# Moving the last S5 scan, its readout and its relay behind the first attention head

## The chip, the cores and the metric

The kernel runs on one core of a Trainium2 chip. The metric is the device time of one execution in microseconds (us). The kernel before takes 1720.06 us (median of 3 runs, 1719.47 to 1720.97). The engines are named as the profile names them: PE (matmul) with its weight loads PEld, DVE (vector), ACT (scalar), POOL (GpSimd) and SP, which here only issues DMAs. Each engine works through its own list of instructions in order.

## The reference

One layer over 512 tokens of width 1024. Cut to what matters here:

```
proj = rmsnorm(x) @ w_in                       # columns: q, k, v (512 each) and u (512)
att  = chunked_attention(rmsnorm(q), rmsnorm(k), v, rel_bias)      # 8 heads of 64
ssm  = s5_mixer(u)                             # diagonal complex scan, then gelu, then a gate
h    = x + concat(rmsnorm(att), rmsnorm(ssm)) @ w_out
h    = h + memory_attention(rmsnorm(h), rmsnorm(mem))              # 256 memory tokens, 4 heads
h    = h + peer_ffn(rmsnorm(h))                # product-key experts
```

In the mixer, y = Re(C x) + d u is read out of the scanned state x, then `y = gelu(y)` and `y = y * sigmoid(y @ w_glu + b_glu)`. The change touches only the order of work inside the mixer, the attention heads and the norm of the memory; what is computed stays the same.

## The kernel before

The program has a front (norm, projections, S5, attention, memory attention) and the expert part. The change lies in the front, between about 137 and 320 us of the span; the expert part fills the rest.

Large products in single precision are made of three passes: `load_split` (L97) brings a weight tile in (tile `wraw`, SP queue, 3 buffers), ACT rounds it (`whi`, L108), DVE or POOL forms the rest (`wlo`, L110), and PE runs L124 to L126 on them (4 buffers of `whi` and of `wlo`). A weight buffer comes free when the last product that reads it is done.

The S5 scan works in four quarters, `scan(0)` to `scan(3)` (L466). A quarter is eight small products into two PSUM banks (`pb`, L472), some sixteen DVE instructions (multiplications L479 to L484, eight `tensor_tensor_scan` L487, multiplications L491 to L496), and the scanned state `XX`. `readout(q)` (L498) is twelve products (`py`, L504 to L506) and a copy on ACT into `Ug` (L507). `relay` (L511) sends `Ug` through HBM to change its layout: eight DMAs write `Ys` (L515, four from the SP queue, four from ACT's), and one DMA on ACT's queue reads `yT` back (L518). `glu_in` (L632) then runs gelu over `yT` on ACT (L634) and splits it (`yh`, `yl`), and `glu` uses it.

An attention head (`att_head`, L669) is a few score products (`pS`, L684), a DVE step with the bias and the row maximum (L685), exp on ACT (L686), transposes on PE (L689), a copy on DVE (`apt`, L690), products with v (`po`, L694) and a scaling (`att`, L698). `mem_in` (L582) normalises the memory (`norm_T`, L166: a square on ACT, a scaling on DVE, transposes `ntp` on PE, the split `Mh`, `Ml` on ACT and DVE). `mem_k(0)` and `mem_k(1)` multiply it by the two halves of `w_mk` (`pv` from `Mh`, 48 products each), and the result leaves PSUM by ACT: a copy `kN` (L597) and two squares `kj` (L599) for each of two token blocks.

PSUM is handed out by tag: two banks under "g" (`pv`, `pz`, `pk`), two under "s" (`pb`, `py`, `ntp`, `po`), four under "a" (`pS`, `pbc` and transposes). The two banks of `mem_k(1)` are those of `mem_k(0)`, so its first product waits for the `kN` and `kj` of `mem_k(0)`.

What is written first in the program has the higher priority; a scheduler in the compiler fixes each engine's list before the run. The string `PLAN` gives the order from the heads on: digits are heads, m the memory norm, i `glu_in`, g `glu`, k K and v V the halves of the memory keys and values. The scratch tile `xn` of a norm comes from a pool of four tiles (`t4`), which the scan's matrices `MT` and states `XX` use too; `p8` is a pool of four larger tiles, which the transposed input `XT` fills until the product for v is done.

Of the kernel before, what the change touches and what calls it, by code (L numbers as in the profile page):

```python
# [9 lines left out]
F32 = mybir.dt.float32  # L10
# [25 lines left out]
    _o += _w  # L36
NVEC = _o
NB8 = 10
PLAN = 'im012kK34g5v6V7'
POG = 0  # L40
LK = "v"
LV = "gv"
# [16 lines left out]
def setup(tc, es):  # L59
    c = Ctx()  # L60
# [6 lines left out]
    V, S, G, P = c.V, c.S, c.G, c.P  # L67
# [17 lines left out]
    def t4(name, dt=F32, w=1024):  # L85
        return c.tp.tile([128, w], dt, tag="t4", name=name, bufs=4)

    def small(name, shape, dt=F32, bufs=4):
        return c.tp.tile(shape, dt, tag=name, name=name, bufs=bufs)
# [73 lines left out]
        for b, pv in zip(blocks, pvs):  # L163
            evac(b, 0, pv)

    def norm_T(src, blocks, gain, hl, keep=None, gb=None):  # L166
        if gb is None:
            gb = t4("gb")
            nc.sync.dma_start(gb, gain.partition_broadcast(128))
        for b in blocks:  # L170
            xn = t4("xn")
            ss = small("nss", [128, 2])
            S.activation(xn, src(b), AF.Square, accum_out=ss[:, 0:1])
            rpow(ss[:, 1:2], ss[:, 0:1], 1.0 / 1024)
            V.scalar_tensor_tensor(xn, src(b), ss[:, 1:2], gb, op0=OP.mult, op1=OP.mult)  # L175
            if keep:
                keep(b, xn)
            for half in range(2):
                pt = pst("s", "ntp")
                for q in range(4):  # L180
                    k = half * 4 + q
                    P.transpose(pt[:, q * 128:(q + 1) * 128], xn[:, k * 128:(k + 1) * 128], c.ident)
                pt3 = pt.rearrange("p (k t) -> p k t", k=4)
                hi, lo = hl[0].part(half, b), hl[1].part(half, b)
                S.activation(hi, pt3, AF.Copy)
                c.nt_ins = V.tensor_tensor(lo, pt3, hi, op=OP.subtract).ins
# [29 lines left out]
def front(tc, I, c):  # L216
    nc, V, S, G, P, cp, tp = c.nc, c.V, c.S, c.G, c.P, c.cp, c.tp
    pst, t2, t4, small, vc, rpow, mm3, gemmT, gemmN, norm_T = (
        c.pst, c.t2, c.t4, c.small, c.vc, c.rpow, c.mm3, c.gemmT, c.gemmN, c.norm_T)
# [3 lines left out]
    with tc.tile_pool(name="f1", bufs=1) as f1:  # L223
# [15 lines left out]
        gb = b8([128, 1024], "gb")  # L239
# [226 lines left out]
        def scan(q, MT):  # L466
            pb = [pst("s", "pb") for _ in range(2)]
            s_ = slice(q * 4, q * 4 + 4)
            v3 = lambda a: a.rearrange("p (g c) -> p g c", g=4)
            for h in range(2):  # L470
                for z in range(4):
                    P.matmul(pb[h][:, z * 128:(z + 1) * 128], MT[h][:, q % 2 * 4 + z], Ug[:, q * 4 + z], start=True, stop=True)  # L472
            X = t4("XX").rearrange("p (h g c) -> p h g c", h=2, g=4)
            XX.append(X)
            G.memset(X[:, :, :, 0:1], 0.0)
            br, bi = v3(pb[0]), v3(pb[1])
            tr, ti = Tr[:, s_], Ti[:, s_]
            x0, x1, zr_, zi_ = [v3(f(n_)) for n_, f in (("x0", p2), ("x1", p2), ("zr", a2), ("zi", a2))]
            V.tensor_tensor(x0, br, tr, op=OP.mult)  # L479
            V.tensor_tensor(x1, bi, ti, op=OP.mult)  # L480
            V.tensor_tensor(zr_, x0, x1, op=OP.add)
            V.tensor_tensor(x0, bi, tr, op=OP.mult)
            V.tensor_tensor(x1, br, ti, op=OP.mult)
            V.tensor_tensor(zi_, x0, x1, op=OP.subtract)  # L484
            for z in (zr_, zi_):
                for g in range(4):
                    V.tensor_tensor_scan(z[:, g], mag4[:, q * 4 + g:q * 4 + g + 1].broadcast_to([128, 128]), z[:, g], 0.0,  # L487
                                         op0=OP.mult, op1=OP.add)
            n_ = slice(0, 127)
            T = V.tensor_tensor  # L490
            T(x0, zr_, tr, op=OP.mult)  # L491
            T(x1, zi_, ti, op=OP.mult)
            T(X[:, 0, :, 1:128], x0[:, :, n_], x1[:, :, n_], op=OP.subtract)
            T(x0, zr_, ti, op=OP.mult)
            T(x1, zi_, tr, op=OP.mult)
            T(X[:, 1, :, 1:128], x0[:, :, n_], x1[:, :, n_], op=OP.add)  # L496

        def readout(q):  # L498
            py = pst("s", "py")
            for z in range(4):  # L500
                g = q * 4 + z
                X = XX[q]
                o = py[:, z * 128:(z + 1) * 128]
                P.matmul(o, Mx[:, g], Ug[:, g], start=True, stop=False)  # L504
                P.matmul(o, CAr[:, g], X[:, 0, z], start=False, stop=False)
                P.matmul(o, CAi[:, g], X[:, 1, z], start=False, stop=True)  # L506
            S.activation(Ug[:, q * 4:q * 4 + 4].rearrange("p g c -> p (g c)"), py, AF.Copy)  # L507
# [3 lines left out]
        def relay():  # L511
            Ys = c.dr.tile([32, 16, 4, 128], F32, name="Ys")
            for a in range(2):
                for j in range(4):
                    (nc.sync if j % 2 else nc.scalar).dma_start(  # L515
                        Ys.rearrange("(g a) ch j c -> a j ch g c", a=2)[a, j], Ug[64 * a + 16 * j:64 * a + 16 * j + 16])
            yT.append(b8([128, 4, 512], "yT"))
            nc.scalar.dma_start(yT[0], Ys.rearrange("(m g) ch j c -> (g ch) m (j c)", m=4))  # L518
# [11 lines left out]
        for i in range(2):  # L530
# [9 lines left out]
            if i == 0:  # L540
                local()
                MT = min_T(0, Mn)
                scan(0, MT)
            else:
# [4 lines left out]
                MT = min_T(1, Mn)  # L549
# [14 lines left out]
            rhl.append((rh, rl))  # L564
        vN = b8([128, 4, 512], "vN")
        gemmN([[I["w_v"][i] for i in range(4)]], XT, range(4), lambda b, ct, p: S.activation(vN[:, b], p, AF.Copy), leng=V)
        scan(3, MT)
        readout(2)
        readout(3)
        relay()  # L570
        for i, (rh, rl) in enumerate(rhl):
            for m in range(4):
                pbc = pst("a", "pbc")
# [6 lines left out]
        M = []  # L580

        def mem_in():  # L582
            M.extend(pair(c.p8, "M", 256))
            me = c.p8([128, 2, 1024], "me", F32)
            nc.scalar.dma_start(me, I["mem"].rearrange("(b p) d -> p b d", p=128))
            norm_T(lambda b: me[:, b], range(2), I["gkv"], M)

        mkv = {}

        def mem_k(ct):  # L590
            if ct == 0:
                mkv["kN"] = b8([128, 2, 1024], "kN")
                mkv["ks"] = small("ks", [128, 2, 4], bufs=1)
            kN, ks = mkv["kN"], mkv["ks"]

            def ev(b, _, p):
                S.activation(kN[:, b, ct * 512:(ct + 1) * 512], p, AF.Copy)  # L597
                for e in range(2):
                    S.activation(t2("kj")[:, :256], p[:, e * 256:(e + 1) * 256], AF.Square,  # L599
                                 accum_out=ks[:, b, ct * 2 + e:ct * 2 + e + 1])  # L600
            c.gemmK([I["w_mk"][ct * 4 + i] for i in range(4)], M, range(2), ev, leng=LK)
            if ct == 0:
                return
            mkT = mkv["k"] = b8([128, 8, 256], "mkT")
            dg = []
            for b in range(2):
                rk = small("rk", [128, 4])
                rpow(rk, ks[:, b], 1.0 / 256)
                d_ = t2("dg").rearrange("p (h t) -> p h t", h=4)
                V.tensor_tensor(d_, ident.unsqueeze(1).broadcast_to([128, 4, 128]),  # L610
                                rk.unsqueeze(2).broadcast_to([128, 4, 128]), op=OP.mult)
                dg.append(d_)
            for hd in range(4):
                pk = pst("g", "pk")
                for m in range(2):
                    for b in range(2):
                        P.matmul(pk[:, m * 256 + b * 128:m * 256 + (b + 1) * 128], kN[:, b, hd * 256 + m * 128:hd * 256 + (m + 1) * 128],
                                 dg[b][:, hd], start=True, stop=True)
                for m in range(2):
                    S.activation(mkT[:, hd * 2 + m], pk[:, m * 256:(m + 1) * 256], AF.Copy, scale=vc("gmk", m))  # L620

        def mem_v(ct):
            if ct == 0:
                mkv["v"] = b8([128, 2, 1024], "mv")
            c.gemmK([I["w_mv"][ct * 4 + i] for i in range(4)], M, range(2),
                  lambda b, _, p: S.activation(mkv["v"][:, b, ct * 512:(ct + 1) * 512], p, AF.Copy), leng=LV)
# [71 lines left out]
            V.tensor_tensor(att[:, :, h * 64:(h + 1) * 64], po[:, :256].rearrange("p (b d) -> p b d", b=4),  # L698
                            sm[:, 1].unsqueeze(2).broadcast_to([128, 4, 64]), op=OP.mult)

        todo = {"m": mem_in, "i": glu_in, "g": glu, "k": lambda: mem_k(0), "K": lambda: mem_k(1), "v": lambda: mem_v(0), "V": lambda: mem_v(1)}
        for o in PLAN:
            att_head(int(o)) if o.isdigit() else todo[o]()
        sums = small("sums", [128, 4])
# [525 lines left out]
```

## Time and profile before

| | |
|---|---|
| median of 3 runs | 1720.06 us |
| the profiled execution, its own time | 1718.78 us |
| its span, from first to last instruction | 1717.0 us |
| PE busy | 1663.6 us (97%) |
| DVE busy | 1348.9 us (79%) |
| ACT busy | 722.2 us (42%) |
| POOL busy | 687.6 us (40%) |
| mean granted TensorE clock | 0.988 |

A share of busy time is a mean over the whole span. The page's line of PEclk over 40 slices shows tenths of full speed; it stands at 9 nearly everywhere, so what matters for this change is read from windows of the stretch around 140 to 180 us, where the transposed input has been used up, the scan ends and the heads begin. The chain that ended last gives PE 80% of the span and DVE 13%.

### The profile page before, as it was taken

How to read it: one execution, taken by the hardware profiler on the slowest of the kernel's cores; microseconds unless marked ns; L12 is line 12 of the kernel's file. 1: busy time of each engine (PE TensorE's matmuls, PEld its weight loads, DVE VectorE, ACT ScalarE, POOL GpSimd, SP SyncE). 2: the span in 40 equal slices, each digit the busy share in tenths (PEclk: the TensorE clock that was granted, in tenths of full speed). 3: DMA queues.
4: the chain of work that ended last, by engine and by line, in shares of the span. 5: the costliest groups of instructions: out<-in, count | busy, mean ns of one | idle time of the engine just before them, and what ended most of it. 6: DMA issues, size and time to landing. Idle time of an engine off the chain costs nothing.

```text
span 1717.0 us, 24874 instructions
## 1 busy us (share of the span) xinstructions
PE 1663.6 (97%) x8929; PEld 1447.8 (84%) x8929; DVE 1348.9 (79%) x2699; ACT 722.2 (42%) x1185; POOL 687.6 (40%) x598
## 2 busy tenths in 40 slices
PE   7998999999999989999999999999999999999998
PEld 6776778877787879999998999999999999988886
DVE  7989564654579989987797878787778787889977
ACT  4343673433333247887433333333333333333332
POOL 5130032441477854100255545445444444455431
PEclk9998999999999989999999999999999999999999
DMA  6422433220522237777647998998898888899995
GB/s 203 112 57 92 136 117 121 94 86 13 184 96 71 94 130 224 232 239 234 224 146 263 341 348 323 331 335 298 325 325 327 328 326 313 325 333 348 346 402 213
DMA packets 159852, 388.70 MB, mean 226 GB/s; under 512 B 14440, under 2 KB 74856, under 8 KB 159600
## 3 DMA queue, kind: packets, MB, share of 16 engines
q1 hardware_dynamic: 107504, 212.83, 36.7%
q0 software_dynamic: 36864, 134.23, 21.5%
q10 hardware_dynamic: 15360, 40.05, 6.8%
q8 instruction: 70, 1.15, 0.3%
q14 instruction: 54, 0.44, 0.1%
HBM read 351.48 MB, written 35.26 MB: 225 GB/s over the span
## 4 chain that ended last, share of the span: by engine, by line
PE 80%; DVE 13%; DMA 2%; POOL 2%; issue 2%; ACT 1%; SPq 0%; ACTq 0%; DVEq 0%; POOLq 0%
PE acc L1105 28%; PE pa L124 10%; PE pa L126 9%; PE pa L125 9%; PE pw L1036 3%; PE pv L124 3%; PE pv L126 3%; PE pv L125 3%; DMA act<-Ad 1%; DVE ca L900 1%; PE po L694 1%; DVE ex L921 1%; PE pS L684 1%; DVE xn L175 1%; DVE wlo L110 1%
## 5 line engine op out<-in xcount | busy, mean ns | idle before, releaser
L108 ACT ACTIVATE whi<-wraw 128x1024 fp32r<-128x1024 f32 (+1 forms) x332 | 349.1, 1054 | 392.3 <-PE pa L125 204.4
L110 DVE TENSOR_TENSOR wlo<-wraw,whi 128x1024 fp32r<-128x1024 f32 (+1 forms) x278 | 344.1, 1238 | 51.9 <-ACT whi L108 51.6
L124 PE MATMUL pa<-PTh,whi 128*128 128x384 f32 x1024 | 353.9, 346 | 3.2 <-ACT act L1063 3.2
L126 PE MATMUL pa<-PTh,wlo 128*128 128x384 f32 x1024 | 347.3, 339 | 3.8 <-POOL wlo L110 3.8
L125 PE MATMUL pa<-PTl,whi 128*128 128x384 f32 x1024 | 346.4, 338 | 0.0
L974 POOL DMA_INDIRECT vg<-in_peer_v_dram,ei x128 | 184.3, 1440 | 212.4 <-DVE X L975 195.9
L964 POOL DMA_INDIRECT ug<-in_peer_u_dram,ei x128 | 181.2, 1416 | 200.2 <-DVE ug L965 179.3
L1105 PE MATMUL acc<-wlo,ah 128*128 128x512 f32 x768 | 236.8, 391 | 3.4 <-DVE wlo L110 3.4
L1105 PE MATMUL acc<-whi,ah 128*128 128x512 f32 x768 | 236.7, 392 | 0.8 <-ACT whi L108 0.8
L1105 PE MATMUL acc<-whi,al 128*128 128x512 f32 x768 | 236.6, 391 | 0.0
L124 PEld LDWEIGHTS pa<-PTh,whi 128*128 128x128 f32 x1024 | 194.2, 190 | 6.8 <-ACT act L1063 3.5
L126 PEld LDWEIGHTS pa<-PTh,wlo 128*128 128x128 f32 x1024 | 194.2, 190 | 5.1 <-POOL wlo L110 5.1
L125 PEld LDWEIGHTS pa<-PTl,whi 128*128 128x128 f32 x1024 | 194.4, 190 | 3.3
L965 DVE SCALAR_TENSOR_TENSOR ug<-ug,X 128x1024 f32<-128x1024 f32 x128 | 152.9, 1222 | 41.0 <-DMA ug<-in_peer_u_dram,ei 40.8
L1093 ACT ACTIVATE ah<-act 128x384 fp32r<-128x384 f32 x128 | 67.2, 526 | 266.2 <-PE acc L1105 218.5
L1105 PEld LDWEIGHTS acc<-wlo,ah 128*128 128x128 f32 x768 | 144.4, 188 | 35.3 <-DVE wlo L110 3.8
L975 DVE SCALAR_TENSOR_TENSOR X<-vg,dots,X 128x1024 f32<-128x1024 f32 x128 | 164.2, 1283 | 9.6 <-DMA vg<-in_peer_v_dram,ei 5.5
L110 POOL TENSOR_TENSOR wlo<-wraw,whi 128x1024 fp32r<-128x1024 f32 x54 | 131.5, 2443 | 99.8 <-ACT whi L108 99.8
L1105 PEld LDWEIGHTS acc<-whi,al 128*128 128x128 f32 x768 | 144.4, 188 | 31.1
L1105 PEld LDWEIGHTS acc<-whi,ah 128*128 128x128 f32 x768 | 143.3, 188 | 26.4 <-ACT whi L108 1.6
L1039 ACT ACTIVATE stg<-pw 128x256 f32<-128x256 f32 x192 | 104.8, 682 | 27.9 <-PE pw L1036 22.7
L1101 DVE TENSOR_TENSOR al<-act,ah 128x384 fp32r<-128x384 f32 x128 | 72.4, 566 | 37.5 <-ACT ah L1093 37.4
(383 smaller groups left out, 2637.1 us busy)
## 6 DMA issues: line engine op xcount, KB each, us to landing
wraw<-in_ut_dram SPq DMA_DIRECT2D x128, 512.0 KB, 5.4
wraw<-in_peer_v_dram SPq DMA_DIRECT2D x128, 512.0 KB, 6.5
Wd<-stg SPq DMA_DIRECT2D x24, 1024.0 KB, 5.9
wt<-Wd ACTq DMA_DIRECT2D x32, 768.0 KB, 7.7
wraw<-in_w_pq_dram SPq DMA_DIRECT2D x16, 512.0 KB, 3.3
h<-in_x_dram SPq DMA_DIRECT2D x8, 512.0 KB, 6.8
wraw<-in_w_qk_dram SPq DMA_DIRECT2D x8, 512.0 KB, 3.9
wraw<-in_w_mk_dram SPq DMA_DIRECT2D x8, 512.0 KB, 4.2
```

The source lines that it names most:

```text
L108: S.activation(hi, raw, AF.Copy)
L110: ins = leng.tensor_tensor(lo, raw, hi, op=OP.subtract).ins
L124: P.matmul(out, lhs[0], rhs[0], start=first, stop=False)
L125: P.matmul(out, lhs[0], rhs[1], start=False, stop=False)
L126: P.matmul(out, lhs[1], rhs[0], start=False, stop=last)
L964: G.indirect_dma_start(out=ug, out_offset=None, in_=I["peer_u"], in_offset=IOX(ap=ei[:, k:k + 1], axis=0))
L965: V.scalar_tensor_tensor(ug, ug, 1.0, c.X0, op0=OP.mult, op1=OP.mult, accum_out=dots[:, k:k + 1])
L974: G.indirect_dma_start(out=vg, out_offset=None, in_=I["peer_v"], in_offset=IOX(ap=ei[:, k:k + 1], axis=0))
L975: V.scalar_tensor_tensor(a0, vg, dots[:, k:k + 1], a0, op0=OP.mult, op1=OP.add)
L1039: S.activation(stg[e][:, :, q * 8 + hf * 4:q * 8 + hf * 4 + 4].rearrange("p i t -> p t i"), pw.rearrange("p (t i) -> p t i", t=4)[:, :, e ...
L1101: c.v_ins = V.tensor_tensor(al, a, ah, op=OP.subtract).ins
L1105: P.matmul(acc[b * 2 + d], l[:, b * 128:(b + 1) * 128], v[r][:, d * 512:(d + 1) * 512], start=n == 0 and l is ah and r == 0, stop=n == 127 ...
```

## The change

Two edits. First, the last quarter's scan, its readout and the relay leave their place ahead of the heads; they become an entry `s` of the plan, behind head 0, and `glu_in` (i) moves from the first place behind head 2. Second, the memory norm takes the pool `p8` for its gain and its scratch tile: a fourth tile `gx` there holds the gain in one half (loaded over ACT's queue instead of SP's) and the scratch of both blocks in the other half; no `t4` tile is used there any more.

```
-PLAN = 'im012kK34g5v6V7'
+PLAN = 'm0s12ikK34g5v6V7'
...
-    def norm_T(src, blocks, gain, hl, keep=None, gb=None):
+    def norm_T(src, blocks, gain, hl, keep=None, gb=None, xn=None):
...
+        scratch = xn
         for b in blocks:
-            xn = t4("xn")
+            xn = t4("xn") if scratch is None else scratch
...
-        scan(3, MT)
         readout(2)
-        readout(3)
-        relay()
...
-            norm_T(lambda b: me[:, b], range(2), I["gkv"], M)
+            gx = c.p8([128, 2, 1024], "gx", F32)
+            nc.scalar.dma_start(gx[:, 0], I["gkv"].partition_broadcast(128))
+            norm_T(lambda b: me[:, b], range(2), None, M, gb=gx[:, 0], xn=gx[:, 1])
...
-        todo = {"m": mem_in, "i": glu_in, "g": glu, ...}
+        def scan_out():
+            scan(3, MT)
+            readout(3)
+            relay()
+
+        todo = {"s": scan_out, "m": mem_in, "i": glu_in, "g": glu, ...}
```

The lists of the engines differ from about 139 us on and have the same order again from within the product with `w_out` on. Three places follow. Line numbers of the kernel after lie one to five higher or up to two lower than before for the same operation.

ACT, from the relay's read (`yT` from `Ys`) to the first copy of the memory keys (`kN`); `asb` is the exp of a head. Before, the gelu over `yT` stands between exps of heads 0 and 1, and the next exp comes behind `kN`:

```order
L518 DMA yT<-Ys 128x4x512
L686 ACTIVATE asb,asm<-asb,asm 128x256
L686 ACTIVATE asb,asm<-asb,asm 128x512
L634 ACT_TABLE_LOAD
L634 ACTIVATE yT<-yT 128x2048
L636 ACTIVATE yh<-yT 128x512 x4
L108 ACTIVATE whi<-wraw 128x1024
L597 ACTIVATE kN<-pv 128x512
L599 ACTIVATE kj,ks<-pv 128x256 x2
L108 ACTIVATE whi<-wraw 128x1024
L686 ACT_TABLE_LOAD
```

These are the same operations after, with exps of heads 2 and 3:

```order
L519 DMA yT<-Ys 128x4x512
L686 ACTIVATE asb,asm<-asb,asm 128x384
L686 ACTIVATE asb,asm<-asb,asm 128x256
L686 ACTIVATE asb,asm<-asb,asm 128x128
L686 ACTIVATE asb,asm<-asb,asm 128x256
L634 ACT_TABLE_LOAD
L634 ACTIVATE yT<-yT 128x2048
L686 ACT_TABLE_LOAD
L686 ACTIVATE asb,asm<-asb,asm 128x512
L636 ACTIVATE yh<-yT 128x512 x4
L597 ACTIVATE kN<-pv 128x512
L599 ACTIVATE kj,ks<-pv 128x256 x2
```

The gelu stands ahead of the first `kN` in both lists; after, the second table load and one exp have moved between the gelu and `kN`, and the split `whi` of a weight has left that place.

PE, where the readout of a quarter (`py`) meets the score products of the heads (`pS` from `kT`, `qT`). Before, the readouts of quarters 2 and 3 follow the first four score products, and `mem_k(0)` (`pv` from `Mh`) comes behind them:

```order
L575 MATMUL pbc<-rl,selr 128x512
L684 MATMUL pS<-kT,qT 128x512
L684 MATMUL pS<-kT,qT 128x384
L684 MATMUL pS<-kT,qT 128x128
L684 MATMUL pS<-kT,qT 128x512
L504 MATMUL py<-Ug,Mx 128x128
L505 MATMUL py<-XX,CAr 128x128
L506 MATMUL py<-XX,CAi 128x128
```

All 24 products of the two readouts stood there, with eleven transposes, two score products and two GEMM products between. After, the readout of quarter 3 begins behind the second half of that scan's products (`pb`) and the last two products of `mem_k(0)`:

```order
L473 MATMUL pb<-Ug,MT 128x128 x4
L125 MATMUL pv<-wlo,Mh_1429 128x512
L126 MATMUL pv<-whi,Ml_1430 128x512
L505 MATMUL py<-Ug,Mx 128x128
L689 MATMUL pS<-ident,asb 128x128 x4
L694 MATMUL po<-vN,apt 128x64 x4
L684 MATMUL pS<-kT,qT 128x384
L506 MATMUL py<-XX,CAr 128x128
L689 MATMUL pS<-ident,asb 128x128 x3
L684 MATMUL pS<-kT,qT 128x256
L507 MATMUL py<-XX,CAi 128x128
```

What moved in front of it are all 48 products of `mem_k(0)` and the rest of head 0; its products now stand between work of heads 1 and 2. Some 30 rows further on in the list after, `mem_k(1)` begins:

```order
L684 MATMUL pS<-kT,qT 128x128
L694 MATMUL po<-vN,apt 128x64 x3
L684 MATMUL pS<-kT,qT 128x512
L689 MATMUL pS<-ident,asb 128x128 x4
L684 MATMUL pS<-kT,qT 128x256
L124 MATMUL pv<-whi,Mh_1429 128x512
```

Between the readout of quarter 3 and this place the list after holds only work of heads 1 to 4; in the list before, products of `mem_k(0)` and `mem_k(1)` stand between the heads' pieces all the way.

DVE, in the first half of the last quarter's scan (`pb` times the tables `Tr` and `Ti`). Before:

```order
L480 TENSOR_TENSOR x_1379<-pb,Ti 128x512
L481 TENSOR_TENSOR zr<-x_1378,x_1379 128x512
L482 TENSOR_TENSOR x_1378<-pb,Tr 128x512
L483 TENSOR_TENSOR x_1379<-pb,Ti 128x512
L487 SCALAR_TENSOR_TENSOR zr<-mag_387,zr 128x128 x4
L484 TENSOR_TENSOR zi<-x_1378,x_1379 128x512
```

It stood in one piece ahead of head 0's bias steps, and the splits `wlo` of `w_mk` for `mem_k(1)` came much later. After:

```order
L110 TENSOR_TENSOR wlo<-wraw,whi 128x1024
L480 TENSOR_TENSOR x_1523<-pb,Tr 128x512
L110 TENSOR_TENSOR wlo<-wraw,whi 128x1024 x2
L481 TENSOR_TENSOR x_1524<-pb,Ti 128x512
L482 TENSOR_TENSOR zr<-x_1523,x_1524 128x512
L110 TENSOR_TENSOR wlo<-wraw,whi 128x1024
L483 TENSOR_TENSOR x_1523<-pb,Tr 128x512
L484 TENSOR_TENSOR x_1524<-pb,Ti 128x512
L488 SCALAR_TENSOR_TENSOR zr<-mag_387,zr 128x128 x4
L485 TENSOR_TENSOR zi<-x_1523,x_1524 128x512
```

Head 0 and the memory's splits have moved ahead of this place, and the four splits `wlo` for `mem_k(1)` stand among the scan.

## Rows read from the trace of the kernel before

**Rows 1.** Windows of 10 us: busy us (instructions) of each engine, PEclk, DMA share, GB/s
```profile
150.00:160.00 10.00, 5.24 (x8) 1.69 (x7) 9.79 (x18) 0.00 (x0) 0.26 (x2) 0.50 0.14 50
160.00:170.00 10.00, 9.17 (x47) 8.03 (x48) 9.93 (x27) 4.14 (x10) 0.92 (x1) 0.73 0.01 2
```

**Rows 2.** Timeline, PE: start us, us, line, out<-in, forms, xcount [idle before <-releaser]
```profile
142.53 2.05 PE L472 MATMUL pb<-Ug,MT 128*128 128x128 f32 x16
...
149.45 5.79 PE L684 MATMUL pS<-kT,qT 64*128 64x512 f32 x8 [1.60 <-DVE rv L120]
160.01 0.77 PE L504 MATMUL py<-Ug,Mx 128*128 128x128 f32 x2 [4.76 <-DVE x L482]
...
165.26 0.43 PE L504 MATMUL py<-Ug,Mx 128*128 128x128 f32 x2
...
171.81 0.39 PE L506 MATMUL py<-XX,CAi 128*128 128x128 f32 x2
172.03 0.60 PE L182 MATMUL ntp<-ident,xn 128*128 128x128 f32 x4
172.39 0.48 PE L126 MATMUL pv<-whi,Ml 128*128 128x512 f32 x1
...
315.36 1.03 PE L182 MATMUL ntp<-ident,xn 128*128 128x128 f32 x8
```

**Rows 3.** Timeline, PE, in the dense stretch behind
```profile
186.60 2.34 PE L694 MATMUL po<-vN,apt 128*128 128x64 f32 x20
188.87 1.13 PE L684 MATMUL pS<-kT,qT 64*128 64x384 f32 x4
189.93 0.50 PE L125 MATMUL pv<-wlo,Mh 128*128 128x512 f32 x1
...
190.50 0.40 PE L124 MATMUL pv<-whi,Mh 128*128 128x512 f32 x1
190.74 0.40 PE L125 MATMUL pv<-wlo,Mh 128*128 128x512 f32 x1
```

**Rows 4.** Timeline, DVE
```profile
136.68 1.23 DVE L110 TENSOR_TENSOR wlo<-wraw,whi 128x1024 fp32r<-128x1024 f32 x1 [2.40 <-ACT whi L108]
...
153.03 1.28 DVE L175 SCALAR_TENSOR_TENSOR xn<-me,nss,gb 128x1024 f32<-128x1024 f32 x1
...
160.38 1.36 DVE L487 TENSOR_TENSOR_SCAN zr<-mag,zr 128x128 f32<-128x128 f32 x4
161.65 0.67 DVE L484 TENSOR_TENSOR zi<-x,x 128x512 f32<-128x512 f32 x1
162.24 0.68 DVE L685 CUSTOM_DVE_ANT_0 asb<-pS,bt 128x512 f32<-128x512 f32 x1
...
168.72 0.68 DVE L496 TENSOR_TENSOR XX<-x,x 128x508 f32<-128x508 f32 x1
...
169.92 0.68 DVE L186 TENSOR_TENSOR Ml<-ntp,Mh 128x512 fp32r<-128x512 f32 x1
```

**Rows 5.** Timeline, ACT, with the DMA issues on its queue (ACTq)
```profile
172.23 0.60 ACT L507 ACTIVATE Ug<-py 128x512 f32<-128x512 f32 x1 [1.38 <-PE py L506]
...
180.18 0.39 ACTq L518 DMA_DIRECT2D yT<-Ys  x1
...
181.90 0.72 ACT L686 ACTIVATE asb<-asb,asm 128x512 f32<-128x512 f32 x1 [0.25 <-DVE asm L697]
182.73 1.28 ACT L634 ACT_TABLE_LOAD   x1
186.03 1.91 ACT L634 ACTIVATE yT<-yT 128x2048 f32<-128x2048 f32 x1 [2.01 <-DMA yT<-Ys]
187.97 2.19 ACT L636 ACTIVATE yh<-yT 128x512 fp32r<-128x512 f32 x4
...
191.01 0.58 ACT L597 ACTIVATE kN<-pv 128x512 f32<-128x512 f32 x1
...
192.21 1.07 ACT L108 ACTIVATE whi<-wraw 128x1024 fp32r<-128x1024 f32 x1
```

More of the change, by code (lines that the diff above doesn't have):

```diff
@@ L699, in att_head @@
                             sm[:, 1].unsqueeze(2).broadcast_to([128, 4, 64]), op=OP.mult)
-        todo = {"m": mem_in, "i": glu_in, "g": glu, "k": lambda: mem_k(0), "K": lambda: mem_k(1), "v": lambda: mem_v(0), "V": lambda: mem_v(1)}
+        def scan_out():
+            scan(3, MT)
+            readout(3)
+            relay()
+        todo = {"s": scan_out, "m": mem_in, "i": glu_in, "g": glu, "k": lambda: mem_k(0), "K": lambda: mem_k(1), "v": lambda: mem_v(0), "V": lambda: mem_v(1)}
         for o in PLAN:
```

## The prediction

> **What bounds the kernel now.** I read the page's busy shares first, then windows of 10 us, then the timelines of PE, DVE and ACT through the stretch that the change moves. PE bounds the kernel nearly everywhere: behind 172 us it goes without a gap through the heads, the memory keys and the gate. The stretch ahead of that is the exception. In the windows DVE is busy 9.79 and 9.93 of 10 us, while PE has 5.24 busy us in the first, all at a granted clock of 0.50 (the 1.2 GHz level), and a mean of 0.73 in the second [rows 1]. PE's timeline shows why: the score products of the first heads run at half clock, then PE stands for 4.76 us until the scan of quarter 2 is there, and the 24 readout products take it to 172.03 [rows 2]. From 142.53 to 172.03 are 29.5 us, in which PE had 8 `pb`, 8 `pbc`, 24 `py`, 11 transposes, 2 GEMM products and six score products: at the prices below 15.0 us. So 14.5 us are lost there, and the change moves just this work. Quarter 3's state is done at 168.72 + 0.68 = 169.40 [rows 4].
>
> **Prices.** From starts of neighbouring rows. PE: a readout or scan product 0.22 (171.81 to 172.03), a transpose 0.09 (four in 0.36) [rows 2]; a `po` product 0.23 (ten in 2.27), score products 1.06 per 512 columns, a GEMM product 0.24 [rows 3]. DVE: four scan instructions 1.27, a 512-wide step 0.6, and by duration less the 0.09 by which neighbours overlap, a weight split 1.14 and the norm's scaling 1.19 [rows 4].
>
> **When the last quarter's state is there.** First as if DVE never waited. Between 136.68 and the end of this scan, DVE's list after holds everything that it held before, and also four weight splits (4.6), four splits of the memory (2.4), the second norm scaling (1.2), three copies (1.6), four bias steps (1.6) and small ones (0.5): 11.9 us. That gives 169.4 + 11.9 = 181.3.
>
> But it does wait. The fourth of those weight splits stands in the middle of the scan, in front of its second multiplication by `Tr`. It needs `whi`, `whi` needs the buffer that the last weight tile of `mem_k(0)` gives back, and that is read to the end by its last product. PE gets there thus. The first key block is scaled after 4 splits, 11 512-wide steps and two scan groups from 136.68, at about 150.7. From there PE's list holds 48 GEMM products (11.5), score products of 2816 columns (5.8), 26 transposes (2.3), 10 `po` (2.3), 11 `py` (2.4) and 8 `pb` (1.8): 26.1 us. Before, PE worked densely from 160.01 and the products went from 0.43 to 0.22 apart at 165.26, which lost half of 5.25 us [rows 2]; I add that 2.6 once. The last product of `mem_k(0)` then ends at 179.4. ACT's split (1.07 [rows 5]), DVE's (1.14) and what is left of the scan (nine 512-wide steps, two scan groups, four pieces of heads 1 and 2 that stand among them, some result waits: 10.1) follow: 191.8.
>
> That wait is not only DVE's. The readout's first product needs a bank of tag "s", both of which hold the scan's `pb` until DVE has read them; behind it on PE stand transposes, `po` and score products of heads 1 and 2. PE has nearly nothing from 179.4 to 191.8.
>
> **What stands behind the state.** Ten readout products are left: 2.2 us at full clock, 4.3 at half; after twelve empty microseconds I take 3.9. The copy `Ug` is 0.60, and from its end to the gelu the relay took 186.03 - 172.83 = 13.2 us, with ACT waiting for the DMA at the end [rows 5]. The relay keeps its eight DMAs, its read and its queues; `w_glu` loads stand ahead of it on SP, but their buffers come free by 183. The gelu takes 1.94. Behind it ACT's list has the table load for exp (1.28), an exp (0.72 and 0.19 for its sum), `yh` (2.19) and only then `kN` with its squares (191.01 to 192.21: 1.2) [rows 5]. The first product of `mem_k(1)` needs that PSUM bank. So it starts at 191.8 + 3.9 + 0.6 + 13.2 + 1.94 + 1.28 + 0.91 + 2.19 + 1.2 = 217.0. Before, the gelu was over by 188 while PE still had products of `mem_k(0)`, so `kN` came without anyone waiting. From the readout to there PE's list has 26 `po`, 27 transposes and score products of 3456 columns, 15.5 us, and one of the transposes waits for the very exp behind the gelu.
>
> The Trainium skill (ScalarE: Activation LUTs, section "Table sets: the hidden batching unit") says to batch calls by table set, and prices a switch at about 2.7 us; the row shows 1.28, and the measurement decides. By its figure, the load that now stands behind the gelu would cost 1.4 us more, and the forecast would be about 1734.7.
>
> **Until the lists agree again.** Take the transposes of the norm behind `w_out`, at 315.36 in the trace [rows 2]. From 172.03, PE's list before needs 143.3 us to there. After, from the start of `mem_k(1)`, it has 46 GEMM products (11.0), 49 transposes (4.4), 40 `po` (9.2) and 4736 score columns (9.8) less: 34.4, so 108.9 are left. PE has been sparse before that start, so the restart at half clock costs 2.6 again. 217.0 + 108.9 + 2.6 = 328.5, which is 13.1 later. Behind it the order is the same, and PE, which ends everything, is shifted.
>
> **Sum.** The profiled execution took 1718.78 in its own time, 1.28 under the median of the runs. 1718.78 + 13.1 = 1731.9, and with the 1.28, 1733.
>
> The memory norm itself costs nothing: its gain lands some microseconds earlier, and it waits for no `t4` tile. Its two blocks now share one scratch, so the second square waits for the first block's transposes; DVE has about 1.5 us of waits there, ahead of the GEMM products that hide them only in part. I leave them in the range.
>
> **Bounds.** No row shows the clock of the new order. Without any DVE wait and at full clock the state is there at 181.3, the readout takes 2.2 and the restart nothing: the start is 204.8, the end 313.7, 1.7 us earlier than before. If PE is at half clock until 165.3 as it was, 4.7 us are added to 191.8, and 0.4 by the readout: 18 us later. Between them I stay with 191.8, since the wait for the weight buffer stands in the lists, and the rows show the clock down at 150.
>
> **Rivals.** *The move gives what it removes.* If PE is dense from 150.7, DVE never waits (181.3) and the relay is not late for ACT, `mem_k(1)` starts when the heads' 15.5 us are done: 181.3 + 2.2 + 15.5 = 199.0, the end is 307.9, 7.5 us earlier: 1713. For it: half of the 14.5 lost us would come back. Against it: the relay would have to take under 7.4 us instead of 13.2, since 15.5 less the copy `Ug`, gelu, load, exp, `yh` and `kN` leaves no more. It decides in favour of faster from there on. *Gain and loss cancel.* The state is there at 181.3 to 184, because the clock comes back early, but ACT is held by the relay as computed: 1718 to 1722. Against it: `pb` and the split share their waits with PE. *It gets worse.* The half clock holds on, the heads' exps behind the relay's read come late on ACT, and PE's heads go at half clock as well: 18 to 22 us, 1738 to 1742. For it: in the trace the clock did not come back during the 5.79 us of score products at 149.45 [rows 2].
>
> **How the numbers follow.** The forecast (13 us slower, 1726 to 1738 by itself) gets 0.60, the worse case 0.17, the cancelled case 0.12, the faster one 0.11. What a measurement of this kernel can tell from no change is about 0.2%, 3.4 us; so faster 0.11, same 0.12, slower 0.77. The range leaves out the faster case and a little of the worst: 1717 to 1741.
>
> **What would show it.** In the profile after: the last `XX` of the scan at about 192 instead of 169; ACT idle at the gelu, released by the DMA of `yT`, at about 209; the first `pv` of `mem_k(1)` released by ACT's `kj` at about 217, with PE idle ahead of it; a granted clock near 0.5 in parts of 180 to 217; the norm's transposes near 328. It is wrong if the last `XX` comes before 184, or if PE reaches `mem_k(1)` without waiting for ACT.

## The result, and the profile after

The changed kernel takes 1744.15 us (median of 4 runs, 1743.54 to 1745.31), the kernel before on the same chip 1720.51 (4 runs, 1719.47 to 1721.69). The ratio is 1.0142, interval 1.0129 to 1.0154: 23.6 us slower. The forecast was 1733, its range 1717 to 1741. The profiled execution has a span of 1743.5 us.

Where the time went is seen in windows of 10 us. Of the kernel after, columns as in [rows 1]:

```profile
140.00:150.00 10.00, 6.68 (x21) 3.88 (x19) 10.00 (x19) 3.25 (x5) 0.62 (x1) 0.74 0.76 292
150.00:160.00 10.00, 9.23 (x23) 4.98 (x24) 9.39 (x19) 2.50 (x7) 0.14 (x1) 0.50 0.25 77
160.00:170.00 10.00, 10.00 (x56) 8.16 (x55) 3.98 (x8) 3.43 (x7) 0.59 (x2) 0.91 0.09 26
...
180.00:190.00 10.00, 3.54 (x19) 2.67 (x18) 9.82 (x19) 2.93 (x4) 0.00 (x0) 0.79 0.28 79
190.00:200.00 10.00, 8.95 (x31) 6.38 (x30) 7.21 (x19) 3.21 (x10) 0.00 (x0) 0.50 0.01 2
200.00:210.00 10.00, 10.00 (x59) 7.88 (x59) 3.46 (x10) 1.91 (x5) 0.14 (x1) 0.86 0.62 131
210.00:220.00 10.00, 8.68 (x32) 5.54 (x32) 4.64 (x15) 6.74 (x12) 0.29 (x2) 0.65 0.45 159
220.00:230.00 10.00, 10.00 (x26) 5.88 (x27) 5.34 (x14) 6.54 (x21) 0.00 (x0) 0.50 0.01 2
230.00:240.00 10.00, 10.00 (x38) 8.07 (x37) 1.04 (x3) 3.17 (x11) 1.17 (x2) 0.82 0.11 26
```

And of the kernel before the one window that is missing in [rows 1]; from 170 on each of its windows reads 10.00 busy us at 1.00:

```profile
140.00:150.00 10.00, 7.78 (x36) 5.04 (x35) 10.00 (x19) 2.97 (x5) 0.46 (x1) 0.91 0.92 318
```

Take two things from each row: the idle time, 10 less PE's busy time, and what the clock cost, PE's busy time times (1 less PEclk). Before, 140 to 250 us hold 7.8 us of idle time and 5.8 us lost to the clock, 13.6 together. After, it is 12.9 and 23.7, 36.6 together. So the stretch loses 23.0 us more, 17.9 of them by the clock and only 5.1 by idle time; the medians differ by 23.6. A row such as 220 to 230 looks perfect by its busy time; only the clock beside it shows that half of it is lost.

PE's timeline after, columns as in [rows 2]:

```profile
180.92 1.05 PE L473 MATMUL pb<-Ug,MT 128*128 128x128 f32 x8
...
182.04 0.40 PE L126 MATMUL pv<-whi,Ml 128*128 128x512 f32 x1
185.79 0.77 PE L505 MATMUL py<-Ug,Mx 128*128 128x128 f32 x2 [3.35 <-DVE x L483]
189.67 1.12 PE L689 MATMUL pS<-ident,asb 128*128 128x128 f32 x4 [3.12 <-ACT asb L686]
...
197.82 0.79 PE L507 MATMUL py<-XX,CAi 128*128 128x128 f32 x2
198.41 0.64 PE L505 MATMUL py<-Ug,Mx 128*128 128x128 f32 x2
...
211.69 0.65 PE L689 MATMUL pS<-ident,asb 128*128 128x128 f32 x4 [1.12 <-ACT asb L686]
...
215.64 2.07 PE L684 MATMUL pS<-kT,qT 64*128 64x512 f32 x2
...
225.10 2.07 PE L684 MATMUL pS<-kT,qT 64*128 64x512 f32 x2
...
229.30 0.79 PE L124 MATMUL pv<-whi,Mh 128*128 128x512 f32 x1
229.89 0.63 PE L125 MATMUL pv<-wlo,Mh 128*128 128x512 f32 x1
...
233.63 0.39 PE L125 MATMUL pv<-wlo,Mh 128*128 128x512 f32 x1
...
339.39 1.03 PE L183 MATMUL ntp<-ident,xn 128*128 128x128 f32 x8
```

PE stands for 3.35 and 3.12 us ahead of the readout, which then goes at 0.43 a product. After a third gap of 1.12 at 211.69 the heads' pieces run one behind the other, and a score product of 512 columns takes 2.07 us (215.64), where the forecast took 1.06 from [rows 3]. `mem_k(1)` begins at 229.30 with no wait in its row, its products come 0.43 apart until 233.3 and 0.23 apart from then on. The norm's transposes come at 339.39, 315.36 before [rows 2].

DVE after, around the last quarter's scan, as in [rows 4]:

```profile
177.19 0.69 DVE L480 TENSOR_TENSOR x<-pb,Tr 128x512 f32<-128x512 f32 x1
179.99 2.59 DVE L110 TENSOR_TENSOR wlo<-wraw,whi 128x1024 fp32r<-128x1024 f32 x2 [2.11 <-ACT whi L108]
182.50 0.68 DVE L481 TENSOR_TENSOR x<-pb,Ti 128x512 f32<-128x512 f32 x1
...
183.82 1.22 DVE L110 TENSOR_TENSOR wlo<-wraw,whi 128x1024 fp32r<-128x1024 f32 x1
...
194.31 0.68 DVE L497 TENSOR_TENSOR XX<-x,x 128x508 f32<-128x508 f32 x1
```

The state is there at 194.31 + 0.68 = 194.99, against 169.40 [rows 4]. The fourth split (183.82) does stand in the scan, but DVE has no idle time in front of it. The scan's second multiplication (182.50) needs the second half of `pb`, which PE issues at 180.92 among the last products of `mem_k(0)`. In this run DVE was at the second and third split until 182.5, and had waited 2.11 us for them, so these rows alone do not tell which of the two holds the state; e2 and e14 below do.

ACT after, against [rows 5]:

```profile
202.49 0.60 ACT L508 ACTIVATE Ug<-py 128x512 f32<-128x512 f32 x1 [3.39 <-PE py L507]
...
216.48 1.91 ACT L634 ACTIVATE yT<-yT 128x2048 f32<-128x2048 f32 x1 [1.10 <-DMA yT<-Ys]
218.62 1.28 ACT L686 ACT_TABLE_LOAD   x1 [0.24 <-DVE asm L685]
...
220.64 2.17 ACT L636 ACTIVATE yh<-yT 128x512 fp32r<-128x512 f32 x4
222.72 0.57 ACT L597 ACTIVATE kN<-pv 128x512 f32<-128x512 f32 x1
...
223.82 0.20 ACT L599 ACTIVATION_READ_ACCUMULATOR kj<-pv 128x1 f32 x1
```

The order is the one that the list showed: gelu (1.10 us of waiting for the relay's read), table load, exp, `yh`, and only then `kN`. The first bank of `mem_k(1)` is free at about 224.

### The profile page after: what moved, and what is told of

Same layout as the page of the kernel before. It is cut to its first block, busy times and chain, and to the rows that moved or that the text cites. A ratio compares the mean times of both kernels' runs of the same rounds, so it can differ in the third digit from the quotient of the medians.

```text
span 1743.5 us, 24877 instructions
## 1 busy us (share of the span) xinstructions
PE 1681.3 (96%) x8929; PEld 1458.1 (84%) x8929; DVE 1351.3 (78%) x2699; ACT 721.1 (41%) x1183; POOL 700.0 (40%) x598
## 4 chain that ended last, share of the span: by engine, by line
PE 66%; DVE 13%; issue 7%; DMA 7%; POOL 4%; ACT 1%; ACTq 0%; DVEq 0%; SPq 0%; POOLq 0%
PE acc L1110 18%; PE pa L124 8%; PE pa L126 8%; PE pa L125 8%; DMA vg<-in_peer_v_dram,ei 5%; POOL vg L979 3%; PE pw L1041 3%; PE pv L124 3%; PE pv L126 2%; PE pv L125 2%; PE pS L684 1%; DMA act<-Ad 1%; PE po L694 1%; DVE wlo L110 1%; DVE ca L905 1%
## 5 line engine op out<-in xcount | busy, mean ns | idle before, releaser
L110 DVE TENSOR_TENSOR wlo<-wraw,whi 128x1024 fp32r<-128x1024 f32 (+1 forms) x278 | 344.9, 1241 | 53.4 <-ACT whi L108 52.7
L979 POOL DMA_INDIRECT vg<-in_peer_v_dram,ei x128 | 192.8, 1506 | 208.1 <-DVE X L980 190.4
L980 DVE SCALAR_TENSOR_TENSOR X<-vg,dots,X 128x1024 f32<-128x1024 f32 x128 | 164.3, 1284 | 18.1 <-DMA vg<-in_peer_v_dram,ei 13.7
```

Source lines behind the costliest of these rows:

```text
L110: ins = leng.tensor_tensor(lo, raw, hi, op=OP.subtract).ins
L979: G.indirect_dma_start(out=vg, out_offset=None, in_=I["peer_v"], in_offset=IOX(ap=ei[:, k:k + 1], axis=0))
L980: V.scalar_tensor_tensor(a0, vg, dots[:, k:k + 1], a0, op0=OP.mult, op1=OP.add)
```

## The experiments

Times come from several runs on one chip, beside the kernel before. In the traces, what lies ahead of the changed stretch varies by up to 6 us from one profiled execution to another, and each count below comes from one of them, so I count from the first `pbc` on PE (140.47 before, 140.45 after, 146.29 in e10): "XX" to the start of the scan's last instruction, "keys" to the first product of `mem_k(1)` where a gap in the products shows it, and "excess" to the norm's transposes, less the 174.9 us of the kernel before. "Idle + clock" is the account from 140 to 250 us of each trace.

| run | median us | ratio to before (interval) | XX | keys | idle + clock | excess |
|---|---|---|---|---|---|---|
| before | | | 28.3 | | 7.8 + 5.8 | 0 |
| after | 1744.2 | 1.0142 (1.0129 to 1.0154) | 53.9 | 88.9 | 12.9 + 23.7 | 24.0 |
| e1 gelu late | 1736.0 | 1.0088 (1.0061 to 1.0114) | 53.9 | 72.0 | 12.5 + 13.9 | 13.8 |
| e2 splits on POOL | 1742.3 | 1.0134 (1.0114 to 1.0154) | 54.9 | 90.8 | 14.1 + 23.0 | 24.2 |
| e3 other bank | 1737.3 | 1.0088 (1.0062 to 1.0115) | 48.3 | 82.9 | 8.5 + 20.0 | 16.6 |
| e4 filled gap | 1745.2 | 1.0141 (1.0119 to 1.0164) | 52.8 | 88.2 | 9.8 + 19.6 | 22.7 |
| e5 scratch only | 1721.3 | 1.0008 (0.9993 to 1.0024) | 28.1 | | 6.4 + 7.6 | 0.1 |
| e6 move only | 1746.7 | 1.0168 (1.0138 to 1.0198) | 58.6 | 92.0 | 13.5 + 24.2 | 26.7 |
| e7 bank, gelu | 1726.8 | 1.0045 (1.0030 to 1.0060) | 49.6 | 64.7 | 8.0 + 10.7 | 6.5 |
| e8 heavier heads | 1741.7 | 1.0129 (1.0109 to 1.0150) | 55.2 | 84.1 | 15.0 + 14.7 | 21.7 |
| e9 e7, POOL | 1728.2 | 1.0051 (1.0038 to 1.0064) | 53.8 | 69.8 | 14.2 + 11.6 | 9.8 |
| e10 scan first | 1721.4 | 1.0004 (0.9991 to 1.0016) | 29.1 | | 6.4 + 5.4 | 0.3 |
| e11 before, POOL | 1722.8 | 1.0017 (1.0008 to 1.0027) | 29.0 | | 9.7 + 5.8 | 1.9 |
| e12 e10, POOL | 1723.0 | 1.0021 (1.0012 to 1.0031) | 31.0 | | 5.4 + 8.7 | 2.5 |
| e13 e7, splits behind | 1727.1 | 1.0038 (1.0022 to 1.0053) | 44.7 | 62.8 | 6.4 + 12.0 | 6.9 |
| e14 splits behind | 1736.1 | 1.0086 (1.0061 to 1.0110) | 52.7 | 84.6 | 12.5 + 18.0 | 16.9 |

**Which edit.** e5 is the scratch alone, e6 the move alone.

```diff
 e5: -PLAN = 'm0s12ikK34g5v6V7'   +PLAN = 'im012kK34g5v6V7'
     and scan(3), readout(3), relay() back ahead of the heads
 e6: -norm_T(..., None, M, gb=gx[:, 0], xn=gx[:, 1])
     +norm_T(..., I["gkv"], M)
```

> The second edit alone: scan, readout, relay and gelu stand where they stood before, the memory norm takes gain and scratch from p8. If the loss comes from the moved scan, 1717 to 1724. Rival: the shared scratch delays the memory's second block (DVE waits of 1.64, 1.78 and 0.67 us at 161 to 166 in the kernel after) and with it mem_k(0), 1725 to 1732.

> The first edit alone: the scan stands behind head 0, the memory norm has its scratch in t4 as before. If the loss comes from the moved scan, 1740 to 1748. Rival as for the scratch alone: 1733 to 1739. It could also be above 1750, since the norm's t4 tiles now compete with the scan's matrices and states.

The scratch costs nothing that can be measured; the move is the whole loss. Without the new scratch it is, if anything, larger: the state then comes 4.7 us later still.

**kN behind the gelu.** e1 puts the gelu behind `mem_k(1)`.

```diff
-PLAN = 'm0s12ikK34g5v6V7'
+PLAN = 'm0s12kK3i4g5v6V7'
```

> Plan m0s12kK3i4g5v6V7: the gelu stands behind mem_k(1), so the first kN stands ahead of the gelu on ACT and no longer waits for the relay. Theory 'chain' (the relay, gelu, table load, exp and yh in front of kN hold mem_k(1) back): mem_k(1) starts at 207 to 212 instead of 229.3, the time falls to 1722 to 1728. Theory 'clock' (PE is late because it works at half clock from 185 to 203 and from 213 to 233, and ACT's kN only fills time that PE would lose anyway): mem_k(1) follows the heads' pieces that are left in front of it at half clock, the gain is 5 us or less, 1739 or more.

PE, the first product of `mem_k(1)`:

```profile
213.18 0.50 PE L124 MATMUL pv<-whi,Mh 128*128 128x512 f32 x1 [0.60 <-ACT kj L599]
```

It starts 16.9 us earlier, counted from `pbc`, and the second stretch at half clock is gone: with products of `mem_k(1)` among the heads the clock reads 1.00 from 210 to 230. The excess falls by 10.2 us. The theory "chain" is close on the start (213.18, expected at 207 to 212), but the time, 1736.0, lies between the ranges of the two theories: the state and the readout are as late as in the kernel after, and 13.8 us stay.

**What holds the state.** e2 moves the four splits to POOL, e3 gives `pb` other banks, e14 keeps the splits on DVE but behind the last `XX`.

```diff
 e2: -c.gemmK(..., range(2), ev, leng=LK)
     +c.gemmK(..., range(2), ev, leng=G if ct else LK)
 e3: -pb = [pst("s", "pb") for _ in range(2)]
     +pb = [pst(tag, "pb") for _ in range(2)]     # tag "a" in scan(3)
 e14: +with tc.issue_after(c.xx_ins):   # the last XX; for ct == 1 only
      +    ins = leng.tensor_tensor(lo, raw, hi, op=OP.subtract).ins
```

> The four splits wlo for mem_k(1) go from DVE to POOL; nothing else changes. Theory 'split' (as predicted: the fourth split waits for the buffer that the last product of mem_k(0) gives back, and sits in the scan): the last XX comes 8 to 11 us earlier, at about 185, the time falls to 1733 to 1736. Theory 'list' (the second half of the scan's products pb stands on PE behind 14 products of mem_k(0) and runs at 180.92 whatever DVE does): the last XX comes 1 to 2 us earlier, the time stays at 1741 to 1744.

> The last scan's two pb banks come from tag a instead of s, so that both halves of its products run ahead of most of mem_k(0) instead of behind it. Theory 'list' (the place of the second half on PE decides when the state is ready): the last XX comes at 178 to 186 instead of 195, PE's gap from 182.5 to 197 shrinks, and with it the half clock; 1726 to 1736. Theory 'split': the fourth split still sits in the scan and waits for mem_k(0) to end, the last XX stays behind 188 and the time within 5 us of 1744.

> The kernel after with the same order of the splits alone (banks and plan unchanged). As predicted before the result (the fourth split's wait for the weight buffer decides when the state is there): the last XX starts at 183 to 187 instead of 194.31, 1730 to 1737. If the second half of pb, behind mem_k(0)'s products on PE, decides: the splits leave only their own 1.6 us, the last XX starts at 192 to 194, 1740 to 1744.

In e2 the time, 1742.3, is the one that went with "list". The state came 1.0 us later, not earlier: DVE waits there for `pb` as well (4.65 us), and POOL's splits slow it (both rows are in the last section).

DVE in e14, where no split is left in the scan:

```profile
177.65 0.69 DVE L484 TENSOR_TENSOR x<-pb,Tr 128x512 f32<-128x512 f32 x1 [0.52 <-PE pb L477]
183.00 0.69 DVE L485 TENSOR_TENSOR x<-pb,Ti 128x512 f32<-128x512 f32 x1 [4.66 <-PE pb L477]
...
193.79 0.68 DVE L501 TENSOR_TENSOR XX<-x,x 128x508 f32<-128x508 f32 x1
```

DVE now stands idle for 4.66 us in the middle of the scan, released by PE's `pb`: the place of the second half in PE's list decides, not the split, and the state comes only 1.2 us earlier. In e3, with both halves early, it comes 5.6 us earlier, although the splits are still there. By its own expectation e3 alone decides nothing: the last `XX` starts at 189.4, behind the 178 to 186 of "list", and the time, 1737.3, lies between the two ranges. With `pb` early the splits are the next thing: DVE has no idle time from 173 to 191, and e13 below takes them out.

e14's time, 1736.1, lies in the range that went with the split, but the state that went with it is not there: the gain of 7 us has another source. Its list has more of the heads ahead of `mem_k(1)`, and the clock stayed up to 220; that the gain comes from there is argued, not tested. Windows of 2 us:

```profile
214.00:216.00 2.00, 2.00 (x14) 1.57 (x14) 0.66 (x3) 1.98 (x5) 0.00 (x0) 1.00 0.61 167
...
218.00:220.00 2.00, 1.19 (x4) 0.29 (x2) 0.42 (x1) 1.99 (x4) 0.00 (x0) 1.00 0.37 90
...
222.00:224.00 2.00, 2.00 (x8) 1.02 (x6) 2.00 (x6) 2.00 (x8) 0.00 (x0) 0.50 0.00 0
```

From 201 to 218 PE has only heads' pieces with hardly a gap, at 1.00; after 0.8 us of idle time in 218 to 220 the clock is at 0.50, with PE busy all the time.

**Is it the clock?** e4 fills the first gap with products of zeros, e8 adds a product of zeros to each score product of heads 2 and 3; both leave the sums as they were.

```diff
 e4: +for j in range(20):   # behind the last product of mem_k(0)
     +    P.matmul(pv[:, 0:128], c.X0[:, 0:128], Tr[:, j % 16], start=False, stop=j == 19)
 e8: +if h in (2, 3):   # behind the score product
     +    P.matmul(pS[:, o:o + n], c.X0[:, 0:128], Tr[:, 0:n // 128]..., start=False, stop=True)
```

> Twenty products of zeros with a table (128 columns, 4.4 us at full clock) are added to the sum of mem_k(0) behind its last product, in PE's first gap (182.5 to 185.8); the lists are otherwise those of the kernel after. Theory 'clock': if the granted clock stays at 1.00 through part of 185 to 203, the readout ends up to 5 us earlier and the heads' work in front of mem_k(1) goes at full clock: 1731 to 1738 although PE has 4.4 us more to do; if the second gap (187 to 189.7) lets it fall all the same, 1743 to 1746. Theory 'chain': PE's pace there doesn't matter, 1743 to 1746 with any clock.

> In heads 2 and 3 each score product gets a second product of 128 rows (zeros times a table) added to its sum: about 5 us more for PE at full clock, and some pieces change places. In the kernel after, PE is busy without a gap from 213 to 229 with heads' pieces alone (64 rows of contraction or 64 columns), at a granted clock of 0.50. If it is these light pieces that let the clock stay down, the clock in that stretch rises above 0.8 and the norm's transposes come no later than 342 in spite of the added work: 1740 to 1747. If the clock hangs on the idle time ahead of the stretch alone, it stays at 0.50 there and the added work costs its price at half clock: 1750 or more.

In e4 the clock held 1.00 through 180 to 190, but PE's second wait, for an exp of head 1, was still there:

```profile
180.00:190.00 10.00, 8.20 (x62) 7.56 (x60) 8.76 (x15) 3.27 (x4) 0.00 (x0) 1.00 0.38 120
190.00:200.00 10.00, 7.75 (x26) 5.34 (x27) 8.09 (x22) 3.73 (x12) 0.00 (x0) 0.62 0.00 0
```

`mem_k(1)` started 0.7 us earlier and the time did not change, as the expectation had it for that case. e8 is the clearer one. Windows, and PE where it reaches `mem_k(1)`:

```profile
200.00:210.00 10.00, 9.82 (x62) 7.33 (x61) 4.06 (x15) 2.78 (x9) 0.14 (x1) 0.99 0.67 139
210.00:220.00 10.00, 9.78 (x58) 6.88 (x56) 4.30 (x14) 6.07 (x8) 0.14 (x1) 1.00 0.51 152
```

```profile
223.26 1.11 PE L693 MATMUL pS<-ident,asb 128*128 128x128 f32 x4 [2.46 <-ACT asb L690]
224.46 0.80 PE L124 MATMUL pv<-whi,Mh 128*128 128x512 f32 x1
```

With some 5 us of work added, the clock stays at 1.00 through 220, PE is early and now waits 2.46 us for the exp behind the gelu, `mem_k(1)` starts 4.8 us earlier and the transposes come 2.3 us earlier than after. So PE at half clock was the last one at `mem_k(1)`; with the half clock gone, ACT's chain is left, at 224.5. e8 also moved some pieces, and the gap at 211.69 went with them, so it does not tell which of the two kept the clock up.

**Both together, and the rest.** e7 joins e1 and e3; e9 is e7 with the eight splits on POOL, e13 is e7 with e14's order of the splits.

> The banks of e3_pb_other_bank and the plan of e1_gelu_late together. If the two losses are separate (gap of PE at 182 to 197 with its half clock; mem_k(1) behind gelu with the second half-clock stretch), their gains of 9.5 and 6.8 us at the norm's transposes add up: transposes at 322 to 325, 1726 to 1730. If both take away the same wait, no more than the better one alone: 329 to 331, 1733 to 1737.

> e7_bank_and_gelu, and all eight splits wlo of w_mk go to POOL. In e3_pb_other_bank the four splits for mem_k(1) stand in the scan on a DVE that is busy from 173 to 191 without a gap. If they are the second thing that holds the state, behind the place of pb, the last XX comes at 182 to 187 (192.64 in e7), PE's gap at 182 to 190 closes, and the time falls by 4 to 8 us against e7: 1719 to 1724. If the state hangs on PE's and ACT's parts of the heads, it stays behind 189 and the time at 1725 to 1729.

> e7_bank_and_gelu, with the four splits wlo for mem_k(1) kept on DVE but ordered behind the last XX. Four splits of 1.14 us leave the scan: the last XX starts 4 to 5 us earlier (188 instead of 192.64), and so does the copy of head 1 for which PE waits 3.37 us at 185.66 to 189.03. If PE's gap then closes and the clock stays up, idle time and half clock from 140 to 250 come down from 18.6 to 13 to 16 us: 1718 to 1723. If PE still waits there for exp and copy of head 1, 1725 to 1729.

e7's gains add up: 10.2 and 7.4 alone, 17.5 together, and by the medians against before 8.0 and 6.7 alone, 15.6 together. e9 does not gain the expected 4 to 8 us: its excess is 3.3 us larger than e7's, the medians' ratios (1.0051 and 1.0045) are the same within their intervals, and the state is later by 4.2 us. Its rows show why. POOL, then DVE:

```profile
179.84 10.01 POOL L110 TENSOR_TENSOR wlo<-wraw,whi 128x1024 fp32r<-128x1024 f32 x4 [8.97 <-ACT whi L108]
```

```profile
178.69 1.36 DVE L488 TENSOR_TENSOR_SCAN zr<-mag,zr 128x128 f32<-128x128 f32 x4
...
183.33 7.11 DVE L488 TENSOR_TENSOR_SCAN zi<-mag,zi 128x128 f32<-128x128 f32 x4
```

Four scan instructions of the same form take 1.36 us just before POOL's splits and 7.11 beside them. e13 avoids that, and the state comes 4.9 us earlier than in e7, as expected; PE's gap at 185 is gone and the clock stays up through it. But the time is that of e7 and the account 18.4 us, not the expected 13 to 16, since PE meets its next gap a few us on. PE, and windows:

```profile
190.73 0.33 PE L693 MATMUL pS<-ident,asb 128*128 128x128 f32 x1 [1.12 <-DVE asm L689]
...
203.78 0.77 PE L128 MATMUL pv<-whi,Mh 128*128 128x512 f32 x1
```

```profile
190.00:192.00 2.00, 1.13 (x7) 0.88 (x7) 1.61 (x6) 0.00 (x0) 0.00 (x0) 1.00 0.72 228
...
194.00:196.00 2.00, 2.00 (x10) 1.66 (x10) 1.78 (x6) 1.74 (x5) 0.00 (x0) 0.50 1.01 232
...
202.00:204.00 2.00, 2.00 (x10) 1.85 (x10) 1.12 (x3) 1.26 (x1) 0.00 (x0) 0.50 0.79 267
```

Idle for 1.12 us at 189.6 and 0.50 at 192.5, PE goes on with heads' pieces: from 194 on they go at half clock, until `mem_k(1)`'s products have brought it back at 207.

**The scan in front again.** e10 has plan `sm012kiK34g5v6V7` with e3's banks, e11 is the kernel before with `LK = "g"` (splits of `w_mk` on POOL), e12 is both.

> Plan sm012kiK34g5v6V7 with the scan's pb in tag a and the scratch in p8: scan, readout and relay stand ahead of the memory norm and head 0 again, only written as an entry of the plan, and the gelu stands behind mem_k(0). If the loss comes from the scan standing behind head 0 and the memory norm, the account of idle time and half clock falls back to 13 to 16 us and the time to 1717 to 1723. If it comes from the other bank or from the gelu behind head 2, 1726 or more.

> The kernel before with the splits wlo of w_mk on POOL, which is idle there, instead of DVE (9.79 and 9.93 of 10 us busy from 150 to 170). Three to four splits of 1.14 us leave DVE ahead of the key blocks and the scan: the last XX comes 2 to 4 us earlier, 1715 to 1719. If PE at half clock sets the pace there, or POOL's longer split (2.4 us) is late for mem_k(0), no change: 1719 to 1722.

> e10_scan_first with the splits on POOL. If DVE sets the pace there, 2 to 4 us below e10_scan_first: 1713 to 1719; if not, as e10_scan_first.

e10 has the time of before, and its state comes within 1 us of it: the loss comes from standing behind head 0 and the memory norm, not from the bank, the new scratch or a gelu behind head 2. POOL helps neither (0.17 and 0.21% slower than before; in e11 the state comes 0.7 us later, where 2 to 4 us earlier were expected). No version beat the kernel before.

## Why the prediction was wrong

The direction was right, and ACT's chain behind the readout took the time that was forecast for it. But that chain did not set the start of `mem_k(1)`, forecast at 217.0 and measured at 229.3: PE came last there. Step by step:

- *State.* "191.8", measured 195.0 (+3.2). The last product of `mem_k(0)` ended at 182.4 instead of 179.4: the windows from 150 to 170 lose 4.6 and 0.9 us to the clock, where 2.6 were charged. The reason given, the fourth split's wait for a weight buffer, was wrong (e2, e14): the second half of `pb` stood behind 14 products of `mem_k(0)` on PE. The two come within 2 us of each other, which hid the error in the sum.
- *Readout.* "after twelve empty microseconds I take 3.9", measured 7.5 from the state to `Ug` at 202.49 (+3.6): eleven products stood behind the state, not ten, all at half clock, with transposes and a score product at half clock among them.
- *Copy to gelu.* 13.8 forecast, 14.0 measured. *Gelu to the end of `kj`.* 7.5 forecast, 7.5 measured. Together the chain lets `mem_k(1)` start at 224.0.
- *The heads beside it.* This step failed: "PE's list has 26 `po`, 27 transposes and score products of 3456 columns, 15.5 us" was laid beside the chain at full clock. PE needed 202.5 to 229.3 for it, most of it at half clock, and came last by 5.3 us. The prediction's own sign of error, that PE reaches `mem_k(1)` without waiting for ACT, is what the row at 229.30 shows.
- *Until the lists agree.* 111.5 forecast with the restart, 110.1 measured (-1.4).

3.2 + 3.6 + 0.2 + 5.3 - 1.4 = 10.9, which is the difference between the transposes' 339.4 and the forecast's 328.5. Most of it goes back to the clock: the forecast charged 6.9 us for it at three restarts (2.6, 1.7, 2.6), the account shows 23.7, of which 1.7 lie ahead of 150. The rival "It gets worse", which said that "the half clock holds on" and that "PE's heads go at half clock as well", was the nearest, at 18 to 22 us, and had 0.17. Its evidence stood in [rows 2]: 5.79 us of score products in a row did not bring the clock back. The rivals on the faster side asked for a state at 181 to 184; no run that keeps the scan behind head 0 had it before 186.3 (e13).

The Trainium skill (TensorE: Matmul & The Clock Gate, section "What's actually happening") says that the clock follows how busy PE has been of late. The trace agrees for the gaps ahead of the falls (3.35 us ahead of 185.79, 1.12 us ahead of 211.69), but the window 220 to 230 has PE busy for 10.00 us at 0.50, so busy time as the profile counts it does not settle it. By that rule alone the heads would have been done up to 7 us sooner (an estimate: half of the 13.7 us from 215.64 to 229.30); the measurement decides.

Not settled: whether the clock falls among heads' pieces through the short gap alone. e14 holds 1.00 on them from 201 to 218; in e13 and in the kernel after it falls behind a gap of 1.12 us, while e9 has a gap of 1.34 us right ahead of `mem_k(1)`'s products and reads 1.00 on both sides of it. That 13.7 us of unbroken heads' work stay at 0.50 in the kernel after is seen, not explained.

## What to carry to other kernels

Account for a stretch as idle time plus busy time times (1 less the granted clock), and forecast both: light pieces that were cheap between big products may run at half clock once a moved dependency leaves them alone on PE, as they did here from 215 to 229. Before naming the wait that makes an operand late, look where its producer stands in the list of its own engine: here 14 products stood ahead of it. Work taken off a busy engine has to be priced on the engine that gets it and on what that one disturbs.

## What the runs showed of the hardware

POOL's splits (2.36 us for e2's first one) slow DVE beside them. In e2, POOL and DVE:

```profile
179.60 7.45 POOL L110 TENSOR_TENSOR wlo<-wraw,whi 128x1024 fp32r<-128x1024 f32 x3 [1.84 <-ACT whi L108]
```

```profile
181.59 0.69 DVE L481 TENSOR_TENSOR x<-pb,Ti 128x512 f32<-128x512 f32 x1 [4.65 <-PE pb L473]
182.31 2.54 DVE L482 TENSOR_TENSOR zr<-x,x 128x512 f32<-128x512 f32 x1
...
186.09 2.19 DVE L488 TENSOR_TENSOR_SCAN zr<-mag,zr 128x128 f32<-128x128 f32 x4
```

The addition of two tensors in SBUF takes 2.54 us instead of 0.69, the scan 2.19 instead of 1.36, while multiplications with one operand in PSUM keep their 0.69. The Trainium skill (Perfetto Trace Analysis, section "Optimizing Scalar/DVE Operations") says that the two engines share a read port of SBUF, so that moving work between them may not help; e2, e9, e11 and e12 agree.

In the kernel after, PE's clock came back behind the readout's products (198.4 to 202.5) and on the first ones of `mem_k(1)` (from 229.3), in e13 on the first ones of `mem_k(1)` too (from 203.8). Of the stretches at half clock read here, none ended on heads' pieces alone, though e14 shows such pieces at 1.00 for 17 us.
